# ConvFFN of a two-layer hybrid encoder: three direct column pairs by token group, a fourth pair made direct, up to three norm steps per matmul block, and the down-projection's first weights fetched before the gated rows

## The chip, the cores and the metric

The kernel runs on one core of a Trainium2 chip, as a single launch. The metric is device time in microseconds. TensorE (PE) does the matmuls, VectorE (DVE) and ScalarE (ACT) the elementwise work, GpSimd (POOL) a few small powers and stores, SyncE (SP) issues most loads. Each engine works through its own instructions in the order in which the program gives them, and waits on semaphores for the others.

## What is computed

Two layers run over 1024 new and 64 later frames, laid side by side as T = 1088 tokens of width 1024. The change touches only the second half of each layer: the output projection with its sandwich norms, and the ConvFFN with D_FF = 2816.

```python
mix = jnp.concatenate([og, od], axis=-1).astype(x.dtype) @ w_out
x = x + rms_norm(mix, ln_mix_post)
h = rms_norm(x, ln_ffn_pre)
up = h @ w_ffn_up                                  # 1024 -> 2 * 2816
ext = jnp.concatenate([conv_state.astype(up.dtype), up], axis=1)
c = conv_b
for i in range(CONV_W):                            # CONV_W = 3, along time
    c = c + conv_w[i] * ext[:, i:i + T]
g, u = jnp.split(c, 2, axis=-1)
y = jax.nn.gelu(g, approximate=True) * u
x = x + rms_norm(y @ w_ffn_down, ln_ffn_post)
```

## The kernel before

**Number format and layout.** Everything is feature-major: 128 features on the partitions, tokens along the row. Each float32 operand is kept as a high and a low part (`WH`/`WL` for weights, `XH`/`XL` for activations, `MH`/`ML` for mixer outputs or gated rows), and a product is three passes: high·high, high·low, low·high. Tokens are cut in three groups of 384, 384 and 320 columns (`GROUPS`). One **block** is one 128-feature output tile of one group: 24 matmuls (8 slices of the contraction times 3 passes), written by `fm_block`.

**Weights.** A 128-column weight tile is a **unit**. `fetch` loads it into one of the two halves of `RAW` (SP), `prep` copies it to `WH` (ACT, line 290), and the low part `WL = RAW - WH` follows on DVE (`low_parts`); only then is the unit after the next fetched into the freed half. `want(n)` puts these steps into the queues.

**Norms.** After the eight output-projection blocks of group g (`c_blocks`), `acc_norm(g)` makes PE sum the squares over the partitions (three 1-column matmuls, `PS<-ONE,SQ`), ACT and POOL make the reciprocal root, and PE spreads it over the partitions (three 128-column matmuls, `PS<-IDN,SML`), from where ACT copies it to `RB`. Then `chain(l, g, 1, ...)` runs 16 DVE steps: eight *first-half* steps (scale by `RB`, add the residual, square on ACT, add to `SQ`), a second such norm `x_norm` (`PS<-ONE,SQ`, `PS<-IDN,RS`), and eight *second-half* steps that make `XH` and `XL` of the group. The chain is a Python generator; `pump(n)` after each block writes up to n of its steps into the engines' queues, as long as the planner's own clocks say that DVE is less than 1.5 us behind PE. `need(key)` in front of an up-projection block writes all steps that are still missing at once.

**Up projection.** A *column pair* j is the tile j of the gate half and of the linear half. The first `NC` = 3 pairs are **direct**: six blocks each (2 halves x 3 groups), followed by `ffn_step` (bias, three convolution taps, GELU, product, store to `YD` in memory). Pairs 0 and 1 run group by group, so that group g+1 may still be in its norm; pair 2 follows, over all groups. The other 19 pairs go through `Blocks`, a seven-product Strassen-Winograd form of the 2x2 blocks (features x tokens): 7 products of 24 matmuls with 272 columns each. Its token-side sums come from `fresh(l)`, another generator on DVE and ACT that writes `MH`/`ML`. The raw weights of a pair alternate between `RB`/`SQ` and `RAW` (`Blocks.raw`).

**Down projection.** It runs in chunks of gated rows (`CHUNKS`), the first with j = 0 to 3. Rows are loaded from `YD` (`y_load`), split with `y_high` (ACT, line 1492) and `y_low` (DVE) into `MH`/`ML`; the weights are units again (line 251). In the last pair of `Blocks` (n = blk.n - 1) the code starts this for chunk 0: the rows are staged in `TMP`, `RB` and `SQ`, and the first two weight units are in `held`, so they are not fetched before step i = 4.

Of the kernel before, what the change touches and what calls it, by code (L numbers as in the profile page):

```python
# [21 lines left out]
T = SEQ + DEC  # L22
# [7 lines left out]
O_QG, O_KG, O_VG, O_RG, O_GD, O_QD, O_KD, O_VD = 0, 256, 512, 1024, 1536, 1552, 2064, 2576  # L30
NK = SEQ + PAST + DEC
BIG = 1.0e30
NC = 3
HT = T // 2
Q = HT // 2
NP = 7 * (NF - NC)
SKIPS = (0, 1, 2)
CHUNKS = ((0, 4), (4, 8), (8, 12), (12, 15), (15, 18))


# [11 lines left out]
def hybrid_kernel(ctx: ExitStack, tc: tile.TileContext,  # L52
# [27 lines left out]
    MSK = sb.tile([128, 2, 128], U8, name="MSK")  # L80
    VC = sb.tile([128, DEPTH, 300], F32, name="VC")
    CO = sb.tile([128, 2, 2, 44], F32, name="CO")
    HALO = sb.tile([128, 4, 2], F32, name="HALO")
    ONE = sb.tile([128, 1], F32, name="ONE")
    EPC = sb.tile([128, 1], F32, name="EPC")
    NEGH = sb.tile([128, 4], F32, name="NEGH")
# [139 lines left out]
    def fm_unit(w, c0, slot):  # L226
        return add_unit(lambda raw: nc.sync.dma_start(
            raw[:, :1024].rearrange("p (k c) -> p k c", k=8),
            w[:, c0:c0 + 128].rearrange("(k p) c -> p k c", p=128)), slot)
# [155 lines left out]
    def nxt(k=1):  # L385
        v = sl["n"] % 4
        sl["n"] += k
        return v

    for l in range(DEPTH):  # L390
# [20 lines left out]
        kq(3, (nxt(), nxt()))  # L411
        L["wo"] = [(m, fm_unit(w_out[l], m * 128, nxt())) for m in (0, 1, 2, 3, 4, 5, 6, 7, 0, 1, 2, 3, 4, 5, 6, 7)]
        for j in range(NC):
            L["up", j] = fm_unit(w_ffn_up[l], j * 128, nxt())
            fm_unit(w_ffn_up[l], FF + j * 128, nxt())
        L["prod"] = [nxt() for _ in range(NP)]
        for c, (ja, jb) in enumerate(CHUNKS):
            for m in range(8):
# [828 lines left out]
    def ffn_step(l, new):  # L1247
# [6 lines left out]
        if new is not None:  # L1254
# [2 lines left out]
            u = j + s * NF  # L1257
            fl["n"] += 1
            e = EX[:, fl["n"] % 2]
            hal = HALO[:, 2 * (j % 2) + s]  # L1260
            if g == 0:
                V.memset(e[:, 0:2], 0.0)
            else:
# [73 lines left out]
    class Blocks:  # L1337
# [14 lines left out]
            return (p + self.off) % 4 * 2  # L1352

        def raw(self, n):
            if n % 2 == 0:
                return RB[:, :1024], SQ[:, :1024]
            return RAW[:, :1024], RAW[:, WSLOT:WSLOT + 1024]

# [123 lines left out]
    def y_home(j):  # L1482
        c = next((i for i, (ja, jb) in enumerate(CHUNKS) if ja <= j < jb), 5)
        r = j - (CHUNKS + ((18, NF),))[c][0]
        return ((MH, ML, r), (XH, XL, r), (XH, XL, 4 + r), (MH, ML, r), (XH, XL, r), (MH, ML, r))[c]

    def y_load(j, dst):
        nc.sync.dma_start(dst, YD[j])

    def y_high(j, src):  # L1490
        h, _, r = y_home(j)
        act(h[:, r], src, AF.Copy)  # L1492

    def y_low(j, src):
        h, lo, r = y_home(j)
        V.tensor_tensor(lo[:, r], src, f(h[:, r]), ALU.subtract)

    def ev_dn(first, last, m, g):
        t0, n = GROUPS[g]
# [73 lines left out]
    for l in range(DEPTH):  # L1573
# [168 lines left out]
        def c_blocks():  # L1742
            ring["banks"] = (0, 1, 2, 3, 4, 7)
            for g in range(3):
                residual(g)
            for n, (g, i, w) in enumerate(plan):
                m, u = L["wo"][i]
                if w:
                    want(wo[0] + w)
                fm_block(u, g, wo_rhs, ev_wo(m, g, n % 8 == 0, n % 8 == 7))  # L1750
                yield
                pump()
                if n % 8 == 7:
                    flush()
                    soon(acc_norm(g), ("acc", g))
                    beside(chain(l, g, 1, tag))
# [12 lines left out]
        def up_block(j, s, g):  # L1769
            need((tag, "x", g))  # L1770
            fm_block(L["up", j] + s, g, xrhs, lambda b: ffn_step(l, {"b": b, "j": j, "s": s, "g": g}))

        for g in range(3):
            for j in range(2):
                for s in range(2):
                    up_block(j, s, g)
                    if g == 0 and j == 0:
                        want(L["up", 1] + s)
                    if g == 2 and s + 2 * j in (1, 2):
                        want(L["up", 1] + 1 + s + 2 * j)  # L1780
                    if (g, j, s) == (2, 0, 0):
                        beside(fresh(l))
                    pump(2)
        blk = Blocks(l)
        for j in range(2, NC):
            for g in range(3):
                for s in range(2):
                    up_block(j, s, g)
                    if j + 1 < NC:
                        if g == 0:  # L1790
                            want(L["up", j] + 2 + s)
                    elif (g, s) == (0, 0):
                        blk.load(0)
                    elif (g, s) == (1, 1):
                        blk.prep(0)
                    elif (g, s) == (2, 0):
                        need(("fresh", l))
                        drain()
                        blk.low(0)
                        blk.prep(1)  # L1800
                    pump(2)
        blk.low(1)
        blk.start()
        for p in range(NP):
# [21 lines left out]
                blk.load(n + 2)  # L1826
            if n == blk.n - 1:
                d0 = L["dnc", 0, 0]
                ys = TMP[:, 544:544 + T]
                if i == 0:  # L1830
                    y_load(0, ys)
                elif i == 3:
                    y_high(0, ys)
                    y_low(0, ys)
                    y_load(3, ys)
                elif i == 4:
                    y_load(1, RB)
                    y_load(2, SQ)
                    held.difference_update((d0, d0 + 1))
                    fetch(d0 + 1)  # L1840
                elif i == 5:
                    want(d0)
                    y_high(1, RB)
                    y_low(1, RB)
                elif i == 6:
                    want(d0 + 1)
                    y_high(2, SQ)
                    y_low(2, SQ)
                    y_high(3, ys)
                    y_low(3, ys)  # L1850


        ring["i"] = (2, 4, 0, 0)[blk.bank(NP - 1) // 2]
# [90 lines left out]
```

## Time and profile before

| | us |
|---|---|
| runs | 2861.99, 2852.01, 2853.34 |
| median | 2853.34 |
| profiled execution, device time | 2856.79 |
| its span, first to last instruction | 2855.1 |
| PE busy in the span | 2717.5 |
| DVE busy | 1798.5 |
| ACT busy | 1205.4 |

The chain of waits runs back from the end through PE almost alone; PE is the engine that sets the time, and a stage can only become shorter if PE works less there or waits less. A busy PE isn't a PE at its peak: matmuls count as busy when they run at a lower granted clock, too. So for each stage the length of the stretch, the number of its matmuls and the granted clock are read together.

### The profile page before, as it was taken

What the parts mean: (1) busy time and instruction counts of PE and PEld (TensorE: products, weight loads), DVE (VectorE), ACT (ScalarE), POOL (GpSimd) and SP (SyncE); (2) the same over time, 40 slices, a digit from 0 to 9 for tenths busy, and PEclk for the clock granted to TensorE, in tenths of its full rate; (3) what the DMA queues carried; (4) which work ended last, traced back from release to release, by engine and by line L of the source; (5) the groups of instructions that cost most, each with busy time, mean ns of one, the idle gap of its engine ahead of it and who ended that gap; (6) DMA issues with size and microseconds to landing.
All of it is one profiled execution on the core that took longest, in us unless ns stands there. A gap on an engine that the chain in (4) does not pass through costs nothing. (4 is left out here: it accounts for less than half of the span.)

```text
span 2855.1 us, 48522 instructions
## 1 busy us (share of the span) xinstructions
PE 2717.5 (95%) x19319; PEld 2641.3 (93%) x19319; DVE 1798.5 (63%) x3632; ACT 1205.4 (42%) x2468; POOL 268.4 (9%) x449
## 2 busy tenths in 40 slices
PE   8999989987899999999999999999888999999999
PEld 8999988986899999899999999889778999989998
DVE  5443458466898888345762433674659888873455
ACT  5333358544443343412444342783444343433125
POOL 2200024100000000000021001340000000000000
PEclk9999999997999999999999999999889999999999
DMA  7421274432122222323352214743321222223233
GB/s 247 135 70 52 70 197 116 137 107 66 48 69 83 77 71 80 114 83 101 127 192 79 64 41 121 177 120 111 96 64 50 84 69 90 70 81 116 68 115 130
DMA packets 296618, 284.62 MB, mean 100 GB/s; under 512 B 15374, under 2 KB 264616, under 8 KB 296392
## 3 DMA queue, kind: packets, MB, share of 16 engines
q1 hardware_dynamic: 272328, 214.14, 25.8%
q0 software_dynamic: 17280, 63.58, 6.1%
q10 hardware_dynamic: 6784, 3.81, 0.4%
q8 instruction: 152, 2.49, 0.4%
q14 instruction: 74, 0.61, 0.1%
HBM read 198.85 MB, written 82.62 MB: 99 GB/s over the span
## 5 line engine op out<-in xcount | busy, mean ns | idle before, releaser
L110 PE MATMUL PS<-XH,WL 128*128 128x272 f32 (+2 forms) x3728 | 688.6, 304 | 18.7 <-DVE WL L129 18.7
L110 PEld LDWEIGHTS PS<-XH,WL 128*128 128x128 f32 x3728 | 564.0, 190 | 19.4 <-DVE WL L129 19.1
L110 PE MATMUL PS<-MH,WL 128*128 128x272 f32 (+2 forms) x1936 | 399.7, 305 | 6.3 <-DVE WL L129 6.3
L110 PE MATMUL PS<-XL,WH 128*128 128x384 f32 (+1 forms) x1680 | 401.2, 332 | 0.0
L110 PE MATMUL PS<-XH,WH 128*128 128x384 f32 (+1 forms) x1296 | 335.7, 340 | 23.1 <-ACT XH L513 17.9
L110 PEld LDWEIGHTS PS<-MH,WL 128*128 128x128 f32 x1936 | 300.1, 190 | 6.9 <-DVE WL L129 6.9
L110 PEld LDWEIGHTS PS<-XL,WH 128*128 128x128 f32 x1680 | 301.3, 193 | 0.0
L290 ACT ACTIVATE WH<-RAW 128x1024 fp32r<-128x1024 f32 (+3 forms) x177 | 147.2, 839 | 327.2 <-DMA RAW<-in_w_ffn_down_dram 192.9
L110 PEld LDWEIGHTS PS<-XH,WH 128*128 128x128 f32 x1296 | 232.1, 192 | 36.6 <-ACT XH L513 30.1
L129 DVE TENSOR_TENSOR ACC<-PS,ACC 128x384 f32<-128x384 f32 (+1 forms) x264 | 138.9, 532 | 189.9 <-PE PS L110 189.7
L129 DVE TENSOR_TENSOR WL<-RAW,WH 128x1024 fp32r<-128x1024 f32 (+3 forms) x177 | 167.8, 949 | 130.8 <-ACT WH L290 130.8
L110 PE MATMUL PS<-XL,WL 128*128 128x272 f32 (+2 forms) x1408 | 242.0, 294 | 0.0
L110 PE MATMUL PS<-MH,WH 128*128 128x384 f32 (+1 forms) x720 | 218.3, 335 | 9.4 <-ACT WH L290 4.5
L110 PE MATMUL PS<-ML,WH 128*128 128x384 f32 (+1 forms) x720 | 215.5, 332 | 1.3 <-DVE ML L129 1.3
L1387 ACT ACTIVATE WL<-ACC 128x512 fp32r<-128x512 f32 x152 | 92.2, 629 | 271.7 <-PE PS L110 161.2
L129 DVE SCALAR_TENSOR_TENSOR ACC<-ACC,VC 128x1090 f32<-128x1090 f32 x152 | 204.5, 1346 | 0.1
L110 PEld LDWEIGHTS PS<-XL,WL 128*128 128x128 f32 x1408 | 204.6, 189 | 0.0
L110 PEld LDWEIGHTS PS<-MH,WH 128*128 128x128 f32 x720 | 133.3, 191 | 11.6 <-ACT WH L290 5.0
L110 PEld LDWEIGHTS PS<-ML,WH 128*128 128x128 f32 x720 | 134.4, 191 | 2.8 <-DVE ML L129 2.8
L129 DVE TENSOR_REDUCE SML<-PS 128x1 f32<-128x384 f32 (+6 forms) x144 | 104.2, 724 | 41.8 <-PE PS L110 40.2
L110 PE MATMUL PS<-WH,XH 128*128 128x256 f32 (+1 forms) x864 | 128.4, 291 | 1.2 <-ACT TMP L948 1.2
L110 PE MATMUL PS<-WH,WL 128*128 128x272 f32 x912 | 122.1, 288 | 1.4 <-ACT WL L1387 0.5
(254 smaller groups left out, 4647.5 us busy)
## 6 DMA issues: line engine op xcount, KB each, us to landing
RAW<-in_w_in_dram SPq DMA_DIRECT2D x48, 512.0 KB
RAW<-in_w_ffn_up_dram SPq DMA_DIRECT2D x48, 512.0 KB
YD<-ACC POOLq DMA_DIRECT2D x38, 544.0 KB, 3.0
RAW<-in_w_out_dram SPq DMA_DIRECT2D x32, 512.0 KB
XH<-XS SPq DMA_DIRECT2D x8, 1536.0 KB
RAW<-in_w_ffn_down_dram SPq DMA_DIRECT2D x48, 256.0 KB
RB<-YD SPq DMA_DIRECT2D x22, 544.0 KB
RB<-in_w_ffn_up_dram SPq DMA_DIRECT2D x20, 512.0 KB
```

Source lines behind the costliest of these rows:

```text
L110: nc.tensor.matmul(out, lhsT, rhs, **kw)
L129: return op(out, *a, **kw)
L290: act(hi, src, AF.Copy)
L1387: act(hi, src, AF.Copy)
```

## The change

`NC` goes from 3 to 4: one column pair of each layer moves from `Blocks` to the direct form. Direct pairs 0, 1 and 2 now run group by group (in the last group in the order 2, 0, 1); pair 2's two weight units live in the slots 6 and 7, which are `MH`/`ML`. Pair 3 follows over all groups, and there `Blocks` is set up. `pump` allows three steps in place of one (output projection) or two (up projection). `fresh` is put beside the blocks at the first block of group 2, as before; its steps go out under the same `pump`. `HALO` is widened from two to four pairs. The order of the two raw buffers of `Blocks` is turned round, so that the last pair again uses `RB`/`SQ`. In that last pair, the first two down weights are fetched at step 0, ahead of all gated rows; rows 0 and 2 are loaded then too, row 2 into a free part of `ACC`; rows 1 and 3 at step 4.

```diff
-NC = 3
+NC = 4
-SKIPS = (0, 1, 2)
+SKIPS = (0, 1)
...
         for j in range(NC):
-            L["up", j] = fm_unit(w_ffn_up[l], j * 128, nxt())
-            fm_unit(w_ffn_up[l], FF + j * 128, nxt())
+            a, b = (6, 7) if j == 2 else (nxt(), nxt())
+            L["up", j] = fm_unit(w_ffn_up[l], j * 128, a)
+            fm_unit(w_ffn_up[l], FF + j * 128, b)
...
-            hal = HALO[:, 2 * (j % 2) + s]
+            hal = HALO[:, 2 * (j % 4) + s]
...
         def raw(self, n):
-            if n % 2 == 0:
+            if (self.n - n) % 2:
                 return RB[:, :1024], SQ[:, :1024]
...
+    def like(ap, src):
+        return two(ap) if len(src.shape) > 2 else ap
+
     def y_load(j, dst):
-        nc.sync.dma_start(dst, YD[j])
+        nc.sync.dma_start(dst, like(YD[j], dst))
...
+    def y_both(j, src):
+        y_high(j, src)
+        y_low(j, src)
...
                 fm_block(u, g, wo_rhs, ev_wo(m, g, n % 8 == 0, n % 8 == 7))
                 yield
-                pump()
+                pump(3)
...
+        u0 = L["up", 0]
         for g in range(3):
-            for j in range(2):
+            for i, j in enumerate((0, 1, 2) if g < 2 else (2, 0, 1)):
                 for s in range(2):
                     up_block(j, s, g)
-                    if g == 0 and j == 0:
-                        want(L["up", 1] + s)
-                    if g == 2 and s + 2 * j in (1, 2):
-                        want(L["up", 1] + 1 + s + 2 * j)
-                    if (g, j, s) == (2, 0, 0):
+                    if g == 0 and i < 2:
+                        want(u0 + 2 * i + 2 + s)
+                    if g == 2 and i == 1:
+                        want(u0 + 6 + s)
+                    if (g, i, s) == (2, 0, 0):
                         beside(fresh(l))
-                    pump(2)
+                    pump(3)
         blk = Blocks(l)
-        for j in range(2, NC):
-            for g in range(3):
-                for s in range(2):
-                    up_block(j, s, g)
...
+        for g in range(3):
+            for s in range(2):
+                up_block(3, s, g)
+                if (g, s) == (0, 0):
+                    blk.load(0)
+                elif (g, s) == (1, 1):
+                    blk.prep(0)
+                elif (g, s) == (2, 0):
+                    need(("fresh", l))
+                    drain()
+                    blk.low(0)
+                    blk.prep(1)
+                pump(3)
...
                 d0 = L["dnc", 0, 0]
-                ys = TMP[:, 544:544 + T]
+                ys = (TMP[:, HT:HT + T], two(RB), accv[:, 0:2, HT:], two(SQ))
                 if i == 0:
-                    y_load(0, ys)
-                elif i == 3:
-                    y_high(0, ys)
-                    y_low(0, ys)
-                    y_load(3, ys)
-                elif i == 4:
-                    y_load(1, RB)
-                    y_load(2, SQ)
                     held.difference_update((d0, d0 + 1))
                     fetch(d0 + 1)
+                    for j in (0, 2):
+                        y_load(j, ys[j])
+                elif i == 3:
+                    y_both(0, ys[0])
+                elif i == 4:
+                    y_load(1, ys[1])
+                    y_load(3, ys[3])
+                    y_both(2, ys[2])
                 elif i == 5:
                     want(d0)
-                    y_high(1, RB)
-                    y_low(1, RB)
+                    y_both(1, ys[1])
                 elif i == 6:
                     want(d0 + 1)
-                    y_high(2, SQ)
-                    y_low(2, SQ)
-                    y_high(3, ys)
-                    y_low(3, ys)
+                    y_both(3, ys[3])
```

Three places show how instructions move. The first is PE's queue around the second norm of group 1 in the first layer. Before, the square sums (`PS<-ONE,SQ`) and the spreading (`PS<-IDN,RS`) stand directly behind each other, after the last group-0 block of pair 1 and in front of the first group-1 block:

```order
L110 MATMUL PS<-XH,WH 128x384 x8
L110 MATMUL PS<-XL,WH 128x384 x8
L110 MATMUL PS<-XH,WL 128x384 x8
L110 MATMUL PS<-ONE,SQ 128x1 x3
L110 MATMUL PS<-IDN,RS 128x128 x3
L110 MATMUL PS<-XH,WH 128x384 x8
L110 MATMUL PS<-XL,WH 128x384 x8
```

After, the same norm stands in the output projection of group 2, with a whole block (here the last one, on `MH`, `ML` and the mixer part of `XL`) between its two parts:

```order
L110 MATMUL PS<-ONE,SQ 128x1 x3
L110 MATMUL PS<-MH,WH 128x320 x4
L110 MATMUL PS<-XL,WH 128x320 x4
L110 MATMUL PS<-ML,WH 128x320 x4
L110 MATMUL PS<-XL,WH 128x320 x4
L110 MATMUL PS<-MH,WL 128x320 x4
L110 MATMUL PS<-XL,WL 128x320 x4
L110 MATMUL PS<-IDN,RS 128x128 x3
L110 MATMUL PS<-XH,WH 128x384 x8
```

So the norm moved by five blocks towards the start. Group 2's second norm likewise gets one block between its parts, in the middle of group 1's six blocks.

The second place is DVE's queue where the chain of group 0 begins, early in the output projection of group 1 (first layer). The first-half steps are the pairs `ACC<-ACC,RB` and `ACC<-ACC,VC,XH`, with `SQ<-SQ,TMP` from the third step on; `WL<-RAW,WH` is the low part of a weight unit. Before:

```order
L129 TENSOR_TENSOR ACC<-ACC,RB 128x384
L129 SCALAR_TENSOR_TENSOR ACC<-ACC,VC,XH 128x384
L129 TENSOR_TENSOR WL<-RAW,WH 128x1024
L129 TENSOR_TENSOR ACC<-ACC,RB 128x384
L129 SCALAR_TENSOR_TENSOR ACC<-ACC,VC,XH 128x384
L129 TENSOR_TENSOR WL<-RAW,WH 128x1024
```

After:

```order
L129 TENSOR_TENSOR ACC<-ACC,RB 128x384
L129 SCALAR_TENSOR_TENSOR ACC<-ACC,VC,XH 128x384
L129 TENSOR_TENSOR ACC<-ACC,RB 128x384
L129 SCALAR_TENSOR_TENSOR ACC<-ACC,VC,XH 128x384
L129 TENSOR_TENSOR ACC<-ACC,RB 128x384
L129 SCALAR_TENSOR_TENSOR ACC<-ACC,VC,XH 128x384
L129 TENSOR_TENSOR SQ<-SQ,TMP 128x384
L129 TENSOR_TENSOR WL<-RAW,WH 128x1024
```

Three steps now stand ahead of the weight's low part, where one stood.

The third place is SP's queue at the start of the down projection (first layer). Before, four loads of gated rows (`<-YD`) stand ahead of the first down weight:

```order
L1488 DMA TMP<-YD 128x1088 x2
L1488 DMA RB<-YD 128x1088
L1488 DMA SQ<-YD 128x1088
L251 DMA RAW<-in_w_ffn_down_dram 128x4x128 x5
L1488 DMA RB<-YD 128x1088
```

After:

```order
L251 DMA RAW<-in_w_ffn_down_dram 128x4x128 x2
L1492 DMA TMP<-YD 128x1088
L1492 DMA ACC<-YD 128x2x544
L1492 DMA RB<-YD 128x1088
L1492 DMA SQ<-YD 128x1088
L251 DMA RAW<-in_w_ffn_down_dram 128x4x128 x3
```

The first two weight units moved past all four row loads, and one of the four rows goes to `ACC` in place of a second use of `TMP`.

More of the change, by code (lines that the diff above doesn't have):

```diff
@@ L82, in hybrid_kernel @@
     CO = sb.tile([128, 2, 2, 44], F32, name="CO")
-    HALO = sb.tile([128, 4, 2], F32, name="HALO")
+    HALO = sb.tile([128, 8, 2], F32, name="HALO")
     ONE = sb.tile([128, 1], F32, name="ONE")
@@ L1485, in y_home @@
         return ((MH, ML, r), (XH, XL, r), (XH, XL, 4 + r), (MH, ML, r), (XH, XL, r), (MH, ML, r))[c]
+    def like(ap, src):
+        return two(ap) if len(src.shape) > 2 else ap
     def y_load(j, dst):
-        nc.sync.dma_start(dst, YD[j])
+        nc.sync.dma_start(dst, like(YD[j], dst))
     def y_high(j, src):
         h, _, r = y_home(j)
-        act(h[:, r], src, AF.Copy)
+        act(like(h[:, r], src), src, AF.Copy)
     def y_low(j, src):
         h, lo, r = y_home(j)
-        V.tensor_tensor(lo[:, r], src, f(h[:, r]), ALU.subtract)
+        V.tensor_tensor(like(lo[:, r], src), src, f(like(h[:, r], src)), ALU.subtract)
+    def y_both(j, src):
+        y_high(j, src)
+        y_low(j, src)
     def ev_dn(first, last, m, g):
@@ L1771, in up_block @@
             fm_block(L["up", j] + s, g, xrhs, lambda b: ffn_step(l, {"b": b, "j": j, "s": s, "g": g}))
+        u0 = L["up", 0]
         for g in range(3):
-            for j in range(2):
+            for i, j in enumerate((0, 1, 2) if g < 2 else (2, 0, 1)):
                 for s in range(2):
                     up_block(j, s, g)
-                    if g == 0 and j == 0:
-                        want(L["up", 1] + s)
-                    if g == 2 and s + 2 * j in (1, 2):
-                        want(L["up", 1] + 1 + s + 2 * j)
-                    if (g, j, s) == (2, 0, 0):
+                    if g == 0 and i < 2:
[3 more added lines that the diff above has]
+                    if (g, i, s) == (2, 0, 0):
                         beside(fresh(l))
-                    pump(2)
+                    pump(3)
         blk = Blocks(l)
-        for j in range(2, NC):
-            for g in range(3):
-                for s in range(2):
-                    up_block(j, s, g)
[L1789 to L1801, printed above, removed]
+        for g in range(3):
[11 more added lines that the diff above has]
+                pump(3)
         blk.low(1)
```

## The prediction

> **What bounds the kernel now.** The page comes first, then PE's waits.
>
> ```profile
> span 2855.1 us, 48522 instructions
> PE 2717.5 (95%) x19319; PEld 2641.3 (93%) x19319; DVE 1798.5 (63%) x3632; ACT 1205.4 (42%) x2468; POOL 268.4 (9%) x449
> ```
> ```profile
> PE PS L110 <- DVE SQ L129: 30.6, 5, 8.7
> PE PS L110 <- DVE WL L129: 25.4, 6, 9.3
> PE PS L110 <- ACT XH L513: 17.9, 32, 1.8
> ...
> PE PS L110 <- ACT WH L290: 6.7, 3, 2.5
> ```
>
> PE is busy nearly always and sets the time. The longest waits are for square sums (SQ), weights' low parts (WL) and normed activations (XH). The timeline puts nearly all of these in the FFN, and the windows show what they really cost. First undisturbed stretches (columns: length, busy time with count for PE, PE's weight loads, DVE, ACT, POOL, then granted clock and DMA): four blocks of 384, three of 320, seven Winograd products, and a 384 block with both matmul parts of a norm.
>
> ```profile
> core 0: us, PE busy (x) PEld busy (x) DVE busy (x) ACT busy (x) POOL busy (x), PEclk, DMA share, GB/s
> 706.62:723.29 16.67, 16.67 (x98) 16.67 (x97) 6.87 (x21) 6.95 (x13) 1.08 (x2) 1.00 0.09 34
> 696.06:706.62 10.56, 10.56 (x74) 10.56 (x73) 7.47 (x23) 5.84 (x12) 1.15 (x2) 1.00 0.42 125
> 768.50:789.55 21.05, 21.05 (x171) 21.05 (x169) 20.23 (x44) 9.53 (x12) 0.54 (x1) 1.00 0.24 77
> 553.20:558.62 5.42, 5.42 (x37) 5.42 (x37) 0.00 (x0) 1.97 (x4) 0.87 (x1) 1.00 0.01 3
> ...
> 559.43:614.51 55.08, 55.08 (x357) 55.08 (x357) 36.32 (x58) 28.29 (x56) 3.34 (x4) 1.00 0.42 123
> ```
>
> So a 384 block takes 4.17 us, a 320 block 3.52, a product 3.01, a norm's matmuls 1.25. Now the five disturbed stretches of layer 0, and the sum row of the same five in layer 1 (2027.42 to 2572.83):
>
> ```profile
> 614.51:621.21 6.70, 4.75 (x27) 4.17 (x25) 4.39 (x10) 1.81 (x4) 0.00 (x0) 1.00 0.31 92
> 630.90:658.90 28.00, 16.55 (x62) 13.21 (x62) 19.98 (x43) 11.46 (x22) 2.98 (x4) 0.70 0.24 82
> 667.22:696.06 28.84, 15.57 (x61) 12.61 (x61) 20.94 (x49) 11.09 (x24) 2.94 (x4) 0.64 0.27 86
> 730.32:759.46 29.14, 19.07 (x122) 17.78 (x121) 25.01 (x49) 14.56 (x28) 1.08 (x2) 0.82 0.04 13
> 1144.48:1159.59 15.11, 8.59 (x25) 6.98 (x25) 9.71 (x16) 8.12 (x10) 0.00 (x0) 0.66 0.20 67
> sum 107.79, PE 64.53 PEld 54.74 DVE 80.03 ACT 47.04 POOL 7.00; mean PE 12.91 PEld 10.95 DVE 16.01 ACT 9.41 POOL 1.40
> ```
> ```profile
> sum 108.11, PE 64.80 PEld 55.03 DVE 79.69 ACT 46.92 POOL 7.00; mean PE 12.96 PEld 11.01 DVE 15.94 ACT 9.38 POOL 1.40
> ```
>
> Their work at full clock: (A, first up block) 4.17; (B, norm of group 1) 4.17 + 5.42 = 9.59; (C, norm of group 2) 5.42 + 3.52 = 8.94; (D, start of Winograd) five products, 15.05; (E, start of the down projection) 24 matmuls of 384, 4.17. Excess: A 2.5, B 18.4, C 19.9, D 14.1, E 10.9, together 107.79 - 41.92 = **65.9 us in layer 0 and 66.2 in layer 1, 132.1 in all**. That is more than PE's idle time there (107.79 - 64.53 = 43.3 per layer): after a long wait the matmuls go on at half clock (0.64 to 0.82 on average).
>
> **The change part by part.**
>
> *Fourth direct pair.* Six direct blocks, 2 x (4.17 + 4.17 + 3.52) = 23.7 us, replace seven products, 21.05: **+2.7 per layer**, all on PE. Its two weight units are among the weight parts counted below.
>
> *A, B, C: the norms.* B arises because chain 1 gets one step per block, so `need` issues its rest in one go; PE then stands still for the sums, POOL and the first XH; C is the same for chain 2, and A waits for chain 0's last XH. After the change chain 0 ends seven blocks ahead of the first up block, chain 1 is wholly queued by the second up block, chain 2 by the fifth group-1 block. Is DVE fast enough? Its prices, by spacing:
>
> ```profile
> 637.22 0.55 DVE L129 TENSOR_TENSOR ACC<-ACC,RB 128x384 f32<-128x384 f32 x1
> 637.81 0.62 DVE L129 SCALAR_TENSOR_TENSOR ACC<-ACC,VC,XH 128x384 f32<-128x384 f32 x1
> 638.34 0.55 DVE L129 TENSOR_TENSOR SQ<-SQ,TMP 128x384 f32<-128x384 f32 x1
> 638.81 0.55 DVE L129 TENSOR_TENSOR ACC<-ACC,RB 128x384 f32<-128x384 f32 x1
> ...
> 649.21 0.61 DVE L129 SCALAR_TENSOR_TENSOR ACC<-ACC,VC,RB 128x384 f32<-128x384 f32 x1
> ...
> 650.21 0.61 DVE L129 SCALAR_TENSOR_TENSOR ACC<-ACC,VC,RB 128x384 f32<-128x384 f32 x1
> ```
>
> A first-half step takes 638.81 - 637.22 = 1.59, a second-half step 1.00, so a chain 20.7 (about 17.5 at 320 columns, by width). From chain 0's start (559.43) to the first group-2 block DVE has three chains (59), 14 weight parts at 1.2 (17), 15 square adds at 0.47 (7) and 11 convolution steps at 1.54 (window 706.62: 6.87 less one 0.72 step, over four; 17): 100 us. PE needs 55.1 + 12 x 4.17 + 3 x 1.25 = 109. It fits, at 92%, but not without waits, since DVE's order is fixed. A weight unit's data come 4.1 us after the fetch that its RAW half's release allows (598.17 + 1.22 to 603.46), and ACT stands still until then:
>
> ```profile
> 598.17 1.22 DVE L129 TENSOR_TENSOR WL<-RAW,WH 128x1024 fp32r<-128x1024 f32 x1
> ```
> ```profile
> 603.46 1.06 ACT L290 ACTIVATE WH<-RAW 128x1024 fp32r<-128x1024 f32 x1 [2.58 <-DMA RAW<-in_w_out_dram]
> ```
>
> Walking the four sums that PE must pass: *x_norm(0)*, passed at 558.62 + 4 x 4.17 = 575.3: DVE has 2 x 1.12 + 6 x 1.59, three weight parts, two adds, the last add and the square before it from 559.43, about 577, a wait of 1.5. *acc_norm(1)*: 0.4. *x_norm(1)*, where two weight parts and the square behind a waiting ACT copy come first: 2.3. *acc_norm(2)*, after the first up block: by the same addition unit 16's weight part ends near 615.7 in the new time, so unit 18's data come at 619.8; its ACT copy (1.1), an eviction and the RB copy end at 622.3; then three steps (2.7), a weight part (1.2) and two adds: 627.1, where PE is done at 623.8, a wait of 3.3. x_norm(2): none. Sum 7.5. What do such waits cost beyond themselves?
>
> ```profile
> 1939.46 0.97 PE L110 MATMUL PS<-MH,WH 128*128 128x384 f32 x4 [3.61 <-DVE XL L129]
> ...
> 1945.31 0.85 PE L110 MATMUL PS<-MH,WH 128*128 128x384 f32 x4
> ```
> ```profile
> 2559.91 0.44 PE L110 MATMUL PS<-MH,WH 128*128 128x384 f32 x1 [2.45 <-ACT WH L290]
> ...
> 2563.68 0.69 PE L110 MATMUL PS<-MH,WL 128*128 128x384 f32 x1 [3.16 <-DVE WL L129]
> ```
>
> The 3.61 us wait makes the next block 5.85 long, 1.7 over; E's waits, two of this size close together, cost 4.4 in clock in layer 0 (15.11 - 4.17 less 15.11 - 8.59 idle). I take 2.5, so **10.0 per layer**. Ends: 0 (all hidden) and 19, half of B and C.
>
> The Trainium skill, "TensorE: Matmul & The Clock Gate", section "Part 1: The HAM clock gate", says that the clock halves only after an idle window of about 3.4 us. By that rule my waits, each shorter, would cost nothing in clock and the sum would be 5 lower; E's waits of 2.45 and 3.16 with half clock behind them speak against it.
>
> *D: Winograd's start.* PE waited there for `fresh`, issued in one go because chain 2 had put the planner's DVE clock ahead. One of its four parts takes 731.98 - 727.92 = 4.06:
>
> ```profile
> 727.92 2.23 DVE L129 TENSOR_TENSOR ACC<-ACC 128x544 f32<-128x544 f32 x3
> ...
> 731.98 2.23 DVE L129 TENSOR_TENSOR ACC<-ACC 128x544 f32<-128x544 f32 x3
> ```
>
> Now it runs beside twelve blocks: 16.2, plus 11 convolution steps (17), two weight parts (2.4) and the first parts of `Blocks` (2.1) make 38, against 6 x 3.52 + 4 x 4.17 + 2 x 3.52 = 44.8 on PE, which hides it; without that cover D's 14 come back. I keep **0.5**; ends 0 and 4.
>
> *E: down weights.* The first one stands behind row loads:
>
> ```profile
> 2549.31 0.34 SPq L1488 DMA_DIRECT2D TMP<-YD  x1
> 2549.75 0.38 SPq L1488 DMA_DIRECT2D RB<-YD  x1
> 2550.23 0.37 SPq L1488 DMA_DIRECT2D SQ<-YD  x1
> 2550.66 20.94 SPq L251 DMA_DIRECT2D RAW<-in_w_ffn_down_dram  x4
> ```
> ```profile
> 2559.23 0.63 ACT L290 ACTIVATE WH<-RAW 128x512 fp32r<-128x512 f32 x1 [12.55 <-DMA RAW<-in_w_ffn_down_dram]
> ```
>
> Three rows (1.63 MB) and 0.26 MB take 9.9 us, 190 GB/s; ACT waits 12.55 and everything behind it, the last convolution too. Afterwards the weights and rows 0 and 2 come some 15 us earlier; rows 1 and 3 still start near 2549.75, land after some 3.4 and 6.2 us (estimate from 0.54 MB at that rate plus latency), 2553 and 2556, then ACT 1.1 and DVE 1.3 each: row 3 is complete near 2559, and PE, done with the products at 2559.91 - 2.45 = 2557.46, wants it nine matmuls (1.6) later. Left: **1.0**; ends 0 and 5. The moved loads meet nothing else on SP: the last raw pair was fetched a pair earlier.
>
> *Sum.* Layer 0: -65.9 + 2.7 + 10.0 + 0.5 + 1.0 = -51.7; layer 1: -52.0. The profiled execution took 2856.8 (span 2855.1 and 1.7 around it), 3.4 over the median 2853.3. 2856.8 - 103.7 = 2753.1, and on the median's footing **2750**.
>
> **The rivals.**
>
> *DVE bounds the norms after all.* 92% leaves little; if the walk's waits double with their clock price (the 19 end), time is 2750 + 2 x 9 = 2768. For it: four waits are foreseen already. Against: chain 2 has a whole group of slack. Chance 0.20.
>
> *Short waits leave the clock whole*, so that 2 x 2.5 of clock price goes: 2745. The Trainium skill's "TensorE: Matmul & The Clock Gate", cited above, would have it so. For it: A's 1.95 us of idle (6.70 - 4.75) left the clock at 1.00. Against: E. Chance 0.15.
>
> *The gated rows are late*: row 3 lands behind row 1 on one queue, and half of E stays: 5.5 for 1.0 per layer, 2759. Chance 0.10.
>
> *The change doesn't do what it says*: the planner's clocks hold the steps back, A to D stay, only E goes: 2853 - 2 x (10.9 - 2.7 - 1) = 2839. The three steps do stand in DVE's queue, which speaks against it. Chance 0.03.
>
> *Slower*: weight parts now stand behind three steps (4.8) where one (1.6) stood, 3.2 later, and `RAW` has two halves, so each delay passes to the next fetch but one. A half's round is 4.1 fetch, 1.1 ACT, 1.2 DVE and the queue ahead; with 4.8 ahead in every block 11.2 for two units, 5.6 per unit against PE's 4.17, and PE starves. It decides when three steps stand before most weight parts. Then some 20 units per layer wait 3.2, 64, and half as much again for the clock, 96 in place of the 10 assumed: 2750 + 2 x 86 = 2922. Only two of eight blocks carry three steps before the norm's break, and one each follows. Chance 0.03.
>
> **How the numbers follow.** The forecast itself has the remaining 0.49. With every unknown at its lower end the saving is 132.1 - 5.4 = 126.7, 2726.6; with every one at its upper end (2.7 + 19 + 4 + 5 per layer) 70.7, 2782.6. The range 2725 to 2785 holds all cases but the last two and some margin. A measurement of this kernel tells about 0.5% (14 us) from no change. Faster 0.96, within 0.5% 0.01, slower 0.03.
>
> **What would show it.** Right: B, C and D without waits over 4 us and at clock 1.00 for most of their length; `DVE SQ` as PE's largest wait in the FFN, at acc_norm(2) and x_norm(1); no L290 wait over 3 us for down weights; 12 direct blocks more and 14 products fewer. Wrong: a wait for `WL` inside output-projection blocks (starving), a wait over 4 us at the first product (fresh not hidden), or long `MH`/`ML` waits at the down projection.

## The result, and the profile after

| | us |
|---|---|
| before, four runs | 2850.46 to 2861.99, median 2852.68 |
| changed, four runs | 2738.75 to 2752.91, median 2743.49 |
| ratio, 95% interval | 0.9615 (0.958 to 0.9651) |
| changed, profiled execution | 2747.34 |
| the same kernel in a later comparison, four runs | median 2747.46, ratio 0.9613 (0.959 to 0.9635) |

The changed kernel is 3.9% faster; the forecast was 2750, in a range of 2725 to 2785. From the page of the changed kernel, its first line and the busy times:

```profile
span 2745.6 us, 48446 instructions
PE 2685.3 (98%) x19271; PEld 2626.4 (96%) x19271; DVE 1783.5 (65%) x3632; ACT 1205.2 (44%) x2484; POOL 271.9 (10%) x453
```

PE's waits in the changed kernel (what PE waited for, us in total, times, the longest):

```profile
PE PS L110 <- DVE SQ L129: 15.0, 9, 3.0
...
PE PS L110 <- ACT WH L290: 2.1, 1, 2.1
...
PE PS L110 <- DVE ML L129: 1.8, 2, 0.9
PE PS L110 <- DVE XL L129: 0.8, 1, 0.8
```

The 25.4 us for `WL` and the 17.9 for `XH` are gone, the square sums halved. Where this lies is seen by cutting both executions at the same instructions. The rows below are windows, in order: layer 0 from the last attention transpose to the first Winograd product (**norms' stretch**: the rest of the output projection and the direct blocks), the **products**, the **down projection** up to the sums that follow it; then the stages up to the same transpose of layer 1, and layer 1's three stretches. Before:

```profile
core 0: us, PE busy (x) PEld busy (x) DVE busy (x) ACT busy (x) POOL busy (x), PEclk, DMA share, GB/s
483.96:730.32 246.36, 216.64 (x1287) 206.82 (x1287) 146.93 (x299) 119.11 (x268) 29.94 (x50) 0.92 0.30 93
730.32:1144.48 414.16, 404.09 (x3194) 402.58 (x3192) 366.26 (x675) 164.88 (x226) 10.69 (x20) 0.99 0.23 74
1144.48:1388.55 244.07, 237.55 (x1409) 235.75 (x1409) 119.15 (x191) 67.00 (x100) 0.53 (x1) 0.98 0.36 115
1388.55:1892.91 504.36, 488.36 (x3678) 464.48 (x3677) 262.11 (x584) 238.06 (x621) 88.83 (x145) 0.98 0.38 108
1892.91:2143.32 250.41, 217.06 (x1287) 207.31 (x1288) 147.21 (x299) 119.26 (x268) 29.77 (x50) 0.91 0.30 92
2143.32:2557.48 414.16, 404.11 (x3194) 402.61 (x3192) 366.25 (x675) 164.87 (x226) 10.69 (x20) 0.99 0.23 75
2557.48:2801.80 244.32, 237.44 (x1409) 235.71 (x1410) 119.33 (x191) 71.44 (x108) 0.53 (x1) 0.98 0.34 110
```

After:

```profile
481.73:724.22 242.49, 232.10 (x1431) 228.08 (x1431) 172.46 (x361) 132.26 (x295) 32.82 (x54) 0.97 0.33 102
724.22:1103.05 378.83, 378.83 (x3026) 378.83 (x3025) 337.02 (x619) 155.56 (x211) 9.62 (x18) 1.00 0.24 79
1103.05:1337.52 234.47, 233.58 (x1410) 232.94 (x1409) 115.30 (x184) 63.14 (x97) 0.53 (x1) 1.00 0.37 117
1337.52:1836.19 498.67, 485.12 (x3678) 461.82 (x3677) 262.15 (x584) 237.89 (x621) 88.72 (x145) 0.99 0.39 109
1836.19:2079.44 243.25, 230.82 (x1431) 226.54 (x1431) 172.53 (x361) 132.34 (x295) 32.72 (x54) 0.98 0.33 101
2079.44:2458.28 378.84, 378.84 (x3027) 378.84 (x3026) 337.00 (x619) 155.59 (x211) 9.61 (x18) 1.00 0.25 79
2458.28:2692.73 234.45, 233.56 (x1411) 232.98 (x1410) 115.48 (x184) 67.58 (x105) 0.53 (x1) 1.00 0.35 113
```

The first number of a row is its length. Differences, beside what the prediction's terms give for the same stretch:

| stretch | predicted | layer 0 | layer 1 |
|---|---|---|---|
| norms (A, B, C gone; six blocks more, +23.7; waits +10) | -7.1 | -3.9 | -7.2 |
| products (seven fewer, -21.05; D 14.1 to 0.5) | -34.7 | -35.3 | -35.3 |
| down projection (E 10.9 to 1.0) | -9.9 | -9.6 | -9.9 |

Layer 1's -7.2 holds 3.2 us that no term foresaw. At the start of its output projection PE waited 3.61 us for `XL` before, with one half-clock window of 3.41 us behind that wait (1.7 lost); after, it waits 0.84 there for `XL` and 1.24 for ScalarE, at full clock. What PE waited for in the 3.61 and the 1.24 stands, on ScalarE, behind a weight copy that waits for its load (7.37 us before, 6.48 after). The wait for `XL` is about 3 in the two runs below that have three direct pairs and 0.84 in all with four, so it goes with `NC`. Without these 3.2 the stretch of layer 1 gave -4.0, like layer 0's -3.9, where the terms give -7.1; that layer 1 hits the number is luck. Over both layers the three stretches give -101.2, where -103.7 was predicted. The other 8.3 of the span's 109.5 come from stages whose instructions the change leaves alone (483.96 to 481.73 at the start, 504.36 to 498.67 between the layers, 0.4 at the end); the last run below shows how far these scatter. In the products PE is busy for the whole window at clock 1.00: 18 pairs at 21.05 are 378.9, and the window is 378.83.

What is left in the norms' stretch is seen on PE's timeline (start, us, instruction, and in brackets the wait ahead):

```profile
574.73 0.83 PE L110 MATMUL PS<-ONE,SQ 128*128 128x1 f32 x6 [1.47 <-DVE SQ L129]
...
576.97 1.48 PE L110 MATMUL PS<-ML,WH 128*128 128x384 f32 x4
...
580.54 0.86 PE L110 MATMUL PS<-XL,WL 128*128 128x384 f32 x4
...
615.38 0.83 PE L110 MATMUL PS<-ONE,SQ 128*128 128x1 f32 x6 [2.29 <-DVE SQ L129]
...
627.65 1.15 PE L110 MATMUL PS<-ONE,SQ 128*128 128x1 f32 x6 [2.98 <-DVE SQ L129]
```
```profile
576.88:580.29 3.41, 3.41 (x13) 3.41 (x12) 0.06 (x1) 0.00 (x0) 0.14 (x1) 0.51 0.55 161
...
615.38:623.26 7.88, 7.88 (x53) 7.88 (x54) 3.67 (x6) 3.95 (x8) 1.11 (x1) 1.00 0.75 227
...
627.65:637.00 9.35, 9.35 (x40) 9.35 (x41) 4.73 (x11) 4.04 (x10) 0.85 (x1) 0.63 0.20 57
```

Four matmuls take 0.85 us at full clock and 1.48 in the slow stretch. After the wait of 1.47 us the clock is halved for 3.41 us (the first window); after the longer wait of 2.29 it stays at 1.00 (second); after 2.98 it is halved for most of 9.35 us (third).

### The profile page after: what moved, and what is told of

The parts are those of the page before. It is cut to its first block, busy times and chain, and to the rows that moved or that the text cites. A ratio compares the mean times of both kernels' runs of the same rounds, so it can differ in the third digit from the quotient of the medians.

```text
span 2745.6 us, 48446 instructions
## 1 busy us (share of the span) xinstructions
PE 2685.3 (98%) x19271; PEld 2626.4 (96%) x19271; DVE 1783.5 (65%) x3632; ACT 1205.2 (44%) x2484; POOL 271.9 (10%) x453
## 4 chain that ended last, share of the span: by engine, by line
PE 85%; DVE 5%; DMA 4%; issue 3%; ACT 2%; POOL 0%; SPq 0%; ACTq 0%; DVEq 0%; POOLq 0%
PE PS L110 82%; PE PS L114 3%; DVE ACC L129 2%; DMA RAW<-in_w_out_dram 1%; DVE SML L129 1%; DMA RAW<-in_w_ffn_up_dram 1%; DVE WL L129 1%; DVE SQ L129 1%; ACT WH L290 1%; DMA out_dram<-TMP 0%; DMA WH<-QSd 0%; DVE ML L129 0%; DMA WH<-KSd 0%; ACT ACC L1112 0%; DVE XL L129 0%
## 5 line engine op out<-in xcount | busy, mean ns | idle before, releaser
L110 PE MATMUL PS<-XH,WL 128*128 128x272 f32 (+2 forms) x3600 | 664.3, 303 | 0.0
L110 PEld LDWEIGHTS PS<-XH,WL 128*128 128x128 f32 x3600 | 541.6, 189 | 0.1
L110 PE MATMUL PS<-MH,WL 128*128 128x272 f32 (+2 forms) x1872 | 387.0, 304 | 0.0
L110 PE MATMUL PS<-XH,WH 128*128 128x384 f32 (+1 forms) x1296 | 322.0, 333 | 4.9 <-DVE TMP L129 2.7
L110 PEld LDWEIGHTS PS<-MH,WL 128*128 128x128 f32 x1872 | 289.3, 189 | 0.0
L110 PE MATMUL PS<-XL,WL 128*128 128x272 f32 (+2 forms) x1344 | 230.6, 294 | 0.0
L110 PEld LDWEIGHTS PS<-XL,WL 128*128 128x128 f32 x1344 | 194.7, 188 | 0.0
L129 DVE SCALAR_TENSOR_TENSOR ACC<-ACC,VC 128x1090 f32<-128x1090 f32 x144 | 194.1, 1348 | 0.1
L110 PE MATMUL PS<-WH,XL 128*128 128x256 f32 (+1 forms) x864 | 122.8, 285 | 0.0
```

The lines of the kernel that those rows point to most:

```text
L110: nc.tensor.matmul(out, lhsT, rhs, **kw)
L129: return op(out, *a, **kw)
```

## Experiments

The kernel before was timed again beside each group of runs, with medians of 2852.68 to 2859.74 us. A difference to the changed kernel in us is one of medians; where the two ratios to the kernel before give clearly less, that number stands beside it.

**The steps undone.** Only the number of steps per block goes back.

```diff
-                pump(3)
+                pump()        # output projection
...
-                pump(3)
+                pump(2)       # both up-projection loops
```

> The changed kernel with one norm step per output-projection block and two per up block, as before the change; the third pair by group, the fourth pair and the early down weights stay. My theory (three steps and the third pair are both needed): the second half of each chain is still issued in one go in front of group 1 and group 2, so about half of B and of C comes back, some 10 us each for the 12 that the norm waits of the changed kernel cost, and part of fresh is late, some 6 us: 15 us more per layer, 2773 us. Rival 1 (the third pair by group alone is cover enough): no more than 3 us per layer, 2743 to 2750. Rival 2 (the steps are everything): all of A to D back less the norm waits, 42 us per layer, 2828.

2801.69 us, ratio to the kernel before 0.9809 (0.9793 to 0.9826): 58 us over the changed kernel (55 by the ratios), twice what I expected. Layer 0's windows and PE's waits:

```profile
481.73:742.13 260.40, 239.62 (x1431) 229.90 (x1431) 166.37 (x345) 131.95 (x291) 31.44 (x53) 0.94 0.31 95
742.13:1126.98 384.85, 381.23 (x3026) 379.33 (x3025) 343.62 (x636) 157.83 (x216) 10.19 (x19) 1.00 0.24 78
```
```profile
PE PS L110 <- ACT XH L514: 18.2, 32, 1.8
PE PS L110 <- DVE SQ L129: 12.2, 5, 3.2
```

D returns by 384.85 - 378.83 = 6.0, as expected. The norms' stretch grows by 17.9 (layer 1: 262.71 - 243.25 = 19.5), not by 9. In layer 0 that is 10.4 us more of idle time (260.40 - 239.62 against 242.49 - 232.10) and 7.5 more of PE's time in work, at a clock of 0.94 in place of 0.97. The 32 short waits for `XH` of the kernel before (17.9 us in both layers together) are all back (18.2). I had counted only the wait for the sum as the price of a chain issued late, which did shrink (8.7 to 3.2), and not the row of waits behind it.

**The steps alone**, on the kernel before: `pump()` and `pump(2)` become `pump(3)`, nothing else.

> The kernel before with only the three norm steps per block. My theory (the steps buy A and B; C and D need the third pair and the fourth): per layer A and B, 20.9 us, go less some 8 for the waits that stay at the sums, half of C (10) stays since the second half of chain 2 is issued in one go in front of group 2, and half of D (7) stays: 2853 - 2 x 27 = about 2800 us. Rival 1 (the steps are everything): 2853 - 2 x 42 = 2768. Rival 2 (the steps alone do nothing, since DVE is too full beside two pairs): above 2840.

2789.44 us, ratio 0.9771 (0.975 to 0.9791), 11 under my number. Layer 0's windows:

```profile
485.20:709.72 224.52, 211.61 (x1287) 205.44 (x1287) 157.43 (x315) 121.24 (x272) 30.32 (x50) 0.96 0.33 103
709.72:1112.84 403.12, 401.74 (x3194) 400.21 (x3192) 355.54 (x659) 161.73 (x221) 10.72 (x20) 1.00 0.24 77
```

```profile
PE PS L110 <- DVE SQ L129: 12.8, 9, 2.7
PE PS L110 <- ACT XH L513: 8.0, 14, 1.7
```

The steps alone take 246.36 - 224.52 = 21.8 out of the norms' stretch and leave D at 403.12 - 19 x 21.05 = 3.2 (layer 1: 21.2 and 4.7). The waits for `XH` ahead of the first up block and of group 1 are gone. The 14 that stay, seven in each layer, are those of group 2's first block: in layer 0 it takes 12.2 us from the spreading to the next block (663.27 to 675.46), 8.7 over its 3.52. A, B, rather more than half of C and most of D are thus the steps' work; waits at the sums, with some half clock behind them, take part of the win back.

**The fourth pair taken out**; three pairs by group, three steps and early down weights stay, and `Blocks` is set up in the last group.

```diff
-NC = 4
+NC = 3
...
                     if (g, i, s) == (2, 0, 0):
                         beside(fresh(l))
+                        blk.load(0)
+                    elif (g, i, s) == (2, 1, 1):
+                        blk.prep(0)
+                    elif (g, i, s) == (2, 2, 0):
+                        need(("fresh", l))
+                        drain()
+                        blk.low(0)
+                        blk.prep(1)
...
```

> The changed kernel without the fourth direct pair: three pairs, all by token group, three steps per block, early down weights; Blocks is set up in the last group's blocks. My theory (the fourth pair is the cover of fresh): its 2.7 us per layer are saved, but eleven of fresh's vector operations are issued in one go in front of the first product and D returns, 13 to 14 us per layer: about 2743.5 + 2 x 11 = 2765 us, with WL as the wait at the first products. Rival 1 (chain 2 ends early enough to let fresh finish beside the six 320 blocks, as it nearly does with the steps alone, where 3.1 us of D are left): 2743.5 + 2 x 0.5 = 2744. Rival 2 (fresh is hidden anyway): 2743.5 - 5.4 = 2738.

2761.41 us, ratio 0.9658 (0.9639 to 0.9678): 18 over the changed kernel (12 by the ratios). Windows of layer 0, and PE at the first product:

```profile
481.46:695.81 214.35, 205.35 (x1287) 201.34 (x1287) 152.17 (x307) 119.31 (x270) 30.52 (x50) 0.98 0.34 108
695.81:1105.37 409.56, 404.81 (x3194) 403.31 (x3193) 364.69 (x674) 167.02 (x228) 10.72 (x20) 0.99 0.24 77
```
```profile
700.39 2.18 PE L110 MATMUL PS<-XH,WL 128*128 128x272 f32 x8 [3.41 <-DVE WL L129]
```

D is back with 409.56 - 399.95 = 9.6 (layer 1: 408.00, 8.1) and the wait for `WL` that belongs to it. The fourth pair pays as a cover, not as work saved: it costs 2.7 of PE and hides 8 to 10. It takes the place of the third: with pair 2 behind all groups the steps alone left 3.2 and 4.7 of D, with pair 2 by group they leave 9.6 and 8.1. The norms' stretch without it gives the third pair's own part: 246.36 before, 224.52 with the steps, 214.35 with steps and third pair by group in layer 0; layer 1 has 250.41, 229.23 and 223.42.

**The down projection's start undone**: the first two weight units are again released at step 4, behind the row loads.

```diff
                 if i == 0:
-                    held.difference_update((d0, d0 + 1))
-                    fetch(d0 + 1)
+                    y_load(0, ys)
...
                 elif i == 4:
+                    y_load(1, RB)
+                    y_load(2, SQ)
+                    held.difference_update((d0, d0 + 1))
+                    fetch(d0 + 1)
```

> The changed kernel with the start of the down projection as before the change (row loads ahead of the first two weight units). My theory: E returns whole, 10.9 us per layer in place of about 1.2, so 2743 + 2 x 9.7 = 2763 us, with PE waiting for WH L290 and WL of the down weights again, and nothing else moved. Rival (the fourth pair or the norm steps brought part of it): below 2755.

2767.21 us, ratio 0.9691 (0.9676 to 0.9706). The down projection's window and two of PE's waits:

```profile
1101.45:1345.78 244.33, 237.39 (x1409) 235.60 (x1409) 119.23 (x191) 67.13 (x100) 0.53 (x1) 0.98 0.36 115
```
```profile
PE PS L110 <- ACT WH L290: 6.6, 3, 2.5
PE PS L110 <- DVE WL L129: 6.3, 2, 3.2
```

244.33 - 234.47 = 9.9 us, in layer 1 9.6, and both waits are back: E is this edit alone. The norms' stretch and the products stay within 2.0 of the changed kernel's.

**Two sums a block later**: group 0's second norm and group 2's first.

```diff
-                    soon(x_norm(), (tag, "rs", g))
+                    soon(x_norm(), (tag, "rs", g), 3.0 * (g < 1))
...
-                    soon(acc_norm(g), ("acc", g))
+                    soon(acc_norm(g), ("acc", g), 3.0 * (g > 1))
```

> The changed kernel with two of the four sums that PE waits for put off by one block: the second norm of group 0 and the first norm of group 2. In the changed kernel PE waits 1.5 to 1.7 us and 2.5 to 3.0 us there, and the blocks right behind these waits are 1.6 to 3.1 us longer than the others. My theory (each such wait costs its own length and as much again at a lower clock, and one more block covers it): 4.3 us of waiting and about 3.7 us of slow blocks per layer go, 2743 - 16 = 2727 us. Rival 1 (the slow blocks have another cause than the waits): only the waits go, 2743 - 9 = 2734. Rival 2 (the chain behind is put off and ends late, or the waits move to the next sum): 2743 or more.

2738.39 us, ratio 0.9604 (0.9572 to 0.9636): not told apart from the changed kernel. The norms' window of layer 0:

```profile
480.41:718.44 238.03, 228.95 (x1431) 225.00 (x1431) 172.37 (x361) 132.24 (x295) 32.46 (x54) 0.99 0.33 104
```

The two waits go, but the chains behind move as well, and waits of 1.3 and 1.8 us come up at group 1's first and group 2's second norm. Rival 2 had part of it.

**Low parts on GpSimd**, for the 14 weight units of the norms' stretch.

```diff
-            V.tensor_tensor(*ops, ALU.subtract)
+            (nc.gpsimd if u in pool else V).tensor_tensor(*ops, ALU.subtract)
```

> The changed kernel with the low parts of 14 weight units per layer (those of the norms' stretch) made by GpSimd in place of VectorE: 14 x 1.2 = 17 us off DVE's 100 there. My theory (the waits left at the four sums come from DVE's load): most of the 12 us per layer that waits and slow stretches cost there go, 2743.5 - 2 x 10 = 2723 us. Rival 1 (the waits come from where the plan puts the sums, a block after the last step, whatever the load: the planner then puts the steps and sums earlier and PE waits again): 2740 to 2745. Rival 2 (GpSimd takes so long for a low part that the halves of RAW come free late): PE waits for WL in the output projection, 2760 or more.

2785.29 us, ratio 0.9739 (0.9719 to 0.9759), 42 slower than the changed kernel (35 by the ratios). DVE and POOL at the same moment:

```profile
565.89 3.06 DVE L129 SCALAR_TENSOR_TENSOR ACC<-ACC,VC,XH 128x384 f32<-128x384 f32 x1
...
566.10 2.42 POOL L270 TENSOR_TENSOR WL<-RAW,WH 128x1024 fp32r<-128x1024 f32 x1
```
```profile
484.44:743.84 259.40, 236.56 (x1431) 231.77 (x1432) 175.76 (x347) 132.49 (x295) 65.93 (x68) 0.95 0.31 95
```
```profile
PE PS L110 <- DVE SQ L129: 33.2, 7, 6.9
```

A DVE instruction of 0.62 us takes 3.06 when POOL's begins beside it: 2.44 more, all of POOL's 2.42. Not every low part meets DVE at work. In layer 0's norms' stretch (the window above) DVE is busy for 175.76 us; the changed kernel has 172.46 there, with 14 low parts of 1.22 (17.1) among them. So DVE stood still for some 20 us, 1.5 for each low part that it makes itself in 1.2, and the sums come up to 6.9 us late. My theory isn't tested by this run, since DVE's load rose instead of falling; neither rival named the reason.

**Other sums later, and row 3 early**: group 1's second norm and group 2's first a block later; row 3 loaded with rows 0 and 2 and split ahead of row 1.

> The changed kernel with two edits in separate stages. In the norms: the second norm of group 1 and the first norm of group 2 are put off by one block (in place of the second norm of group 0, as in the run before). In the down projection: row 3 is loaded at step 0 into a free part of ACC and split before row 1, so that only row 1 is loaded late. My theory: waits at the sums move as in the run before, so 2 to 4 us per layer are won in the norms, and the wait of 0.9 for ML at the down projection's start goes (0.9 to 1.3 per layer): 2743.5 - 2 x 4 = 2735 us; the stretch from the first product to the down projection stays at 378.8. Rival 1: the ML wait only moves from row 3 to row 1: 2737. Rival 2 (the later sums push chain 2 into group 2's first block): 2745 or more.

2750.6 us, ratio 0.9621 (0.9602 to 0.9639): nothing won. PE at the norm, and the down projection's window:

```profile
621.87 0.93 PE L110 MATMUL PS<-IDN,RS 128*128 128x128 f32 x6 [2.08 <-POOL RS L437]
```
```profile
1100.44:1337.49 237.05, 235.22 (x1411) 234.47 (x1409) 115.28 (x184) 63.34 (x97) 0.53 (x1) 0.99 0.37 116
```

PE no longer waits for that sum but for its root, although a block stands between sum and spread; the next run shows the same wait and where it comes from. In the down projection the late row is now row 1, which PE reads before row 3, and 234.47 became 237.05. The 0.9 us for `ML` was no matter of when the row landed but of where its split stood in ACT's and DVE's queues.

**Sums in the middle of a block.** All vector steps and the spreads stay where they are; only the three sum matmuls move, to after 12 of the next block's 24. Row 3 is split ahead of the second weight unit's copy.

```diff
                     mm(PS[:, b, :n], wsl(w, u, k * 128, 128), rhs(k, hl, t0, n),
                        start=i == 0, stop=i == 23)
                     i += 1
+                    if i == 12 and st.get("mid") and front and len(front[0]) == 3 and front[0][1] < t1:
+                        front[0].append(1)
+                        step(front)
...
-                    want(d0 + 1)
                     y_both(3, ys[3])
+                    want(d0 + 1)
```

> The changed kernel with the square sums of the norms put into the middle of the next block (after 12 of its 24 matmuls) in place of ahead of it; the spreading stays at that block's end, and all vector steps keep their order. At the down projection's start row 3 is split ahead of the second weight unit's copy. My theory (PE is 0.6 to 3.0 us ahead of DVE at each sum, and each of these waits may also cost one or two stretches of 3.4 us at half clock, 1.7 us each; 2.1 us more of matmuls cover nearly all of it): of 7.3 us of waits and some 5 us of slow stretches per layer about 1.2 stay: 2743.5 - 2 x 11 - 2 x 0.7 = 2720 us, no SQ wait over 1 us in the norms. Rival 1 (DVE is too full there, so the waits move to the spreads or to XH): half of it, 2733. Rival 2 (the slow stretches have another cause than the waits): only the waits go, 2730.

2751.27 us, ratio 0.9621 (0.9602 to 0.9641). In the norms' stretches the waits for sums are down to 0.5 and 0.4, but a new one follows (PE first, then ACT):

```profile
623.56 1.65 PE L110 MATMUL PS<-IDN,RS 128*128 128x128 f32 x6 [4.60 <-POOL RS L441]
```
```profile
621.35 1.06 ACT L290 ACTIVATE WH<-RAW 128x1024 fp32r<-128x1024 f32 x1 [2.50 <-DMA RAW<-in_w_ffn_up_dram]
622.31 0.25 ACT L440 ACTIVATE RS<-PS,EPC 128x3 f32<-128x3 f32 x1
```

This is the wait of the run before, too: ACT's 0.25 us of the norm stand behind a weight copy that waits for its load. At the down projection PE waited 2.5 us for `WL`: the low part of the first unit had slipped behind row 3's split.

**The same, both new waits taken out.**

```diff
+                late = w and any(len(e) == 3 and e[1] <= clock["pe"] for e in front)
-                if w:
+                if w and not late:
                     want(wo[0] + w)
-                fm_block(u, g, wo_rhs, ev_wo(m, g, n % 8 == 0, n % 8 == 7))
+                fm_block(u, g, wo_rhs, ev_wo(m, g, n % 8 == 0, n % 8 == 7),
+                         mid=(lambda w=w: want(wo[0] + w)) if late else None)
...
+                    low_parts()
                     y_both(3, ys[3])
                     want(d0 + 1)
```

> The run with the sums in the middle of a block, with its two new waits taken out. In that run the sums waited for nothing over 0.5 us, but the spread of group 1's second norm came 4.6 and 6.0 us late: ScalarE's first step of the norm stood behind the copy of a weight unit that waited for its load. Here that copy is issued behind the sum, in the blocks where a sum is due. At the down projection the low part of the first weight unit is issued ahead of row 3's split (it had slipped behind it, a wait of 2.5 us). My theory: per layer 7.3 us of waits and some 5 us of slow stretches go but for 1 to 2 us, and 0.7 at the down projection: 2745 - 2 x 11 = 2723 us. Rival 1 (the copies moved by half a block make weights late, a wait for WL in the output projection): above 2740. Rival 2 (slow stretches stay without waits over 1 us): 2730 to 2735.

2730.95 us, ratio 0.9555 (0.9538 to 0.9573); the changed kernel's two ratios are 0.9615 (0.958 to 0.9651) and 0.9613 (0.959 to 0.9635), both intervals above this one. This version is faster than both kernels, by 0.6% more. Windows of the two norms' stretches and of the first down projection, and PE's waits for sums:

```profile
484.07:718.64 234.57, 228.83 (x1431) 224.84 (x1432) 172.33 (x361) 132.37 (x295) 32.50 (x54) 0.99 0.34 105
...
1097.48:1331.43 233.95, 233.44 (x1411) 232.93 (x1409) 115.28 (x184) 63.10 (x97) 0.53 (x1) 1.00 0.37 117
...
1835.48:2072.37 236.89, 227.41 (x1431) 223.30 (x1432) 172.46 (x361) 132.53 (x295) 32.36 (x54) 0.99 0.34 104
```
```profile
PE PS L110 <- DVE SQ L129: 4.3, 5, 1.4
```

242.49 and 243.25 (237.87 and 240.95 in the changed kernel's second profile, below) became 234.57 and 236.89, and 15.0 us of waiting for sums became 4.3. My 2723 assumed that nothing new comes up; waits of 1.05 to 1.30 us for POOL's root stay.

**The changed kernel again**, for a second profile.

> The changed kernel once more, on the same chip as the run beside it and with a second profile. What it tells: which part of the difference between the two profiles is the change and which is the execution. If the 10 us by which the attention stages were shorter after the change (483.96 to 481.73 and 504.36 to 498.67 us, and a wait for XL at layer 1's output projection of 3.61 and 0.84 us) belong to the change, they come out again within 1 us; if they are of the execution, they scatter by some us as they do among the other runs, whose instructions there are the same. Time 2743.5, within 5 us.

2747.46 us. Windows:

```profile
484.21:722.08 237.87, 228.59 (x1431) 224.91 (x1432) 172.44 (x361) 132.50 (x295) 32.72 (x54) 0.99 0.33 104
...
1335.37:1832.15 496.78, 483.38 (x3678) 460.15 (x3677) 262.13 (x584) 238.13 (x621) 89.10 (x145) 0.99 0.39 110
1832.15:2073.10 240.95, 229.23 (x1431) 224.95 (x1432) 172.52 (x361) 132.46 (x295) 32.74 (x54) 0.99 0.33 102
```

The stages that the change leaves alone scatter: the first ends at 479.8 to 485.9 in the twelve profiles, the one between the layers takes 496.8 to 504.4, and the kernel before stands at the long end of the second. I didn't settle why, so I leave the 8.3 us as not shown to be the change's. The norms' stretch itself differs by 4.6 and 2.3 us with the same instructions.

## Why the prediction was right

**What bounds the kernel.** Five disturbed stretches, their excess more than PE's idle time: the sums of waits and clock came back as lengths, stretch by stretch, and undoing a part brought its stretch back.

**Fourth pair, +2.7.** PE's own price holds (seven products off is 21.05, and 378.83 is 18 pairs). Its use lay in D, as the prediction said ("without that cover D's 14 come back"): 9.6 and 8.1 came back, not 14, since the three steps alone hide part of `fresh`.

**A, B, C and the four sums.** The walk along DVE's queue foresaw waits of 1.5, 0.4, 2.3, 3.3 and none; the profile has 1.47, 0.58, 2.29, 2.98 and none, in layer 1 1.70, 0.58, 2.22 and 2.46. **The term that was mis-sized is their clock price**: 2.5 per layer taken, about 5 in this profile (three half-clock windows of 3.41 us in each layer, 1.7 lost in each), so the norm term is about 12 for 10.0. That is 2 of the 3 us by which each layer's stretch, without `XL`, missed -7.1; the rest stays open. In the second profile one and two such windows follow waits of 0.6 to 2.2 us, and the stretches are 8.5 and 6.2 shorter than before, again without `XL`. The price comes in whole steps and by chance, where the prediction treated it as a share of the wait.

**D** is 0 for 0.5. **E**: the first block has 5.51 (1103.05 to 1108.56) for 4.17, 1.3 for 1.0. The step's reason was half right: what is left is row 3, but by the order of its split, not by its landing.

**The sum** gave -103.7 and the three stretches -101.2. Of the latter, 3.2 are the wait for `XL`, which no term held. The median lies 6.5 under the forecast, about the 8.3 us by which the untouched stages were shorter, and these aren't shown to be the change's. The mechanism of each part held; that the sum came out so close is in part luck.

**The rivals.** *DVE bounds the norms after all* (2768): no wait above 3.0. *Short waits leave the clock whole* (2745) came closest in time, for the wrong reason: in this profile they did not leave it whole. The Trainium skill's "TensorE: Matmul & The Clock Gate", section "Part 1: The HAM clock gate", by which only an idle window of about 3.4 us halves the clock, doesn't hold here: 1.47 us did. *The gated rows are late*, *the change doesn't do what it says* and *slower*: no wait for `WL` in the output projection, none over 0.9 at the down projection.

## What to carry to other kernels

A wait on the bounding engine costs its length, the clock behind it, and whatever is issued in one go behind it; price a stretch by its length less its work, not by its waits. Work added to the bounding engine can pay as a cover, and whether it does is seen by taking it out while all else stays. A few small instructions in the middle of a long block (here three sum matmuls) wait less there than ahead of it (4.3 us for 15.0 here), if what they feed doesn't stand behind a waiting copy on the next engine.

## What the runs showed of the hardware

**The clock halves in whole windows, after less than a window of idleness.** In the granted clock of all twelve profiles the half-speed stretches are 3.413 us or a multiple of it (but for the last of each, which ends with the profile), and their starts lie on one grid per execution. The Trainium skill's "TensorE: Matmul & The Clock Gate", section "Part 1: The HAM clock gate", gives this window as 3413 ns and free-running, and that agrees. What decides is how much of a window PE was idle: I laid the grid over the traces and took the windows at full clock, without the program's first 12 us. With 0.4 to 1.3 us of idle time 4 of 270 were followed by half clock, with 1.3 to 1.85 us 49 of 104, with more than 1.85 us 86 of 87. The profile counts the one-column sums behind many of these waits as busy. Counted as idle, they make the step sharper: 3 of 387 windows with 0.4 to 1.3 us, 6 of 82 with 1.3 to 1.75, 130 of 139 above. So about half a window of idle time is enough, and in the changed kernel's first profile a wait of 1.5 to 3 us pays 1.7 us, twice that or nothing. The wait of 2.29 us pays nothing: a line of the grid, at 614.35, cuts it into 1.26 and 1.03. Why the clock came back after one window behind the wait of 1.47 us and after two behind that of 2.98 isn't settled. This much of the norms' stretch changes from one execution to the next.

**GpSimd stops VectorE.** A subtraction of 128x1024 took 2.42 us on POOL and 1.22 on DVE, and a DVE instruction with two operands in on-chip memory stood still for its whole length (3.06 for 0.62). The Trainium skill's "SBUF — State Buffer", section "SBUF: two separate sides", describes the port pair that both share as an exclusive lock, held for a whole instruction, and in that the trace agrees. By the page the instruction that starts first gets it; by the recorded starts DVE's was first here (565.89, POOL's 566.10) and stood all the same.
